# Three dilated attention patterns as one hand-ordered stream of blocks on TensorE, with projections as filler and the merge cut into steps

## The chip, the cores and the metric

The kernel runs on one core of a Trainium2 chip. Five engines work side by side, each through its own queue in order: TensorE (PE in the profile, with PEld for its weight loads), VectorE (DVE), ScalarE (ACT), GpSimd (POOL) and SyncE (SP, which here only issues DMA transfers). The metric is the device time of one execution in microseconds. The kernel before took 1517.27 us, the median of three runs (1516.05 to 1521.16).

## The reference

The kernel computes one hybrid encoder block on 1024 positions of width 1024 in float32. Two attention mixers share one input projection; the change touches the first of them, a mixture of three dilated windows over 8 heads of width 64. Cut to what matters:

```python
DIL_PATTERNS = ((128, 1), (512, 4), (2048, 16))
h = rmsnorm(x, g_mix) * (1 + scale1) + shift1
qa, ka, va, qb, kb, vb, ga, gb = split(h @ w_in)          # ga, gb: the gates
for window, dilation in DIL_PATTERNS:                     # per head
    s = q k^T / 8 + bias ;  m = max(s) ;  p = exp(s - m) ;  l = sum(p)
    o_g = (p / l) v ;  lse_g = m + log(l)
w = softmax over g of lse_g
oa = sum over g of w_g * o_g
ob = neighbourhood attention of qb, kb, vb                # mixer B, 8 heads
merged = sigmoid(ga) * (oa @ w_branch_dil) + sigmoid(gb) * (ob @ w_branch_na)
x = x + gate1 * (merged @ w_out)
# then a convolutional feed-forward layer and the final norm
```

## The kernel before

Positions are stored in the order of their residue modulo 4, so that a dilation of 4 is a contiguous run. The pattern with dilation 4 and the one with dilation 16 are evaluated together on that order (the "near" blocks: 4 residues r, each with 256 queries in two groups g); the pattern with dilation 1 is evaluated on 8 blocks of 128 neighbouring positions, 32 from each residue (the "far" blocks, in four pairs (0,7), (1,2), (3,4), (5,6)). Each float32 product is made of fp32r parts: an operand is split in a high part (ACT) and the rest (DVE or POOL), so a projection of one 128-column tile over 512 positions is 24 matmuls (`product`, lines 77 to 79: 8 values of k times 3). For the scores the two parts of q lie on the two halves of the partitions, and k's high part `ks` and rest `kl` are copied from one half of the partitions to the other by DMA (`k_copies`, line 498) once both halves of a k tile are there. `q_blocks` (line 474) brings q into the block order on POOL.

The heads are handled two at a time ("pairs"). `attend_dil` computes for each head of a pair: scores S into PSUM (lines 609, 610, 639, 640), the bias added and the minimum found by DVE (593), the exponential with its sum by ACT (594), the transposes of P on TensorE (616, 654), the split of the transposed P (ACT 598, DVE 599), the products with V (623, 669), and the evacuation of O (565, 566). Two PSUM buffers hold S, two T, two O and two the projections. After both heads the near and the far results are merged (lines 676 to 711): 16 tiny DVE copies bring the near minima and sums into block order (679), factors are computed on 16 columns (683 to 692), 16 more copies take the near factor back (696), ACT widens each factor (700), TensorE transposes it (704), DVE multiplies (706), POOL adds (710) and SP stores the result (711).

Around it stand the projections of the next pair (`qk_tiles`) and of the gates (`gate_tile`), whose weights SP loads (60), ACT and POOL split (55, 56). In the program they stand behind a pair: `counts = (2, 2, 2, 2, 1, 1, 0, 6)` gate tiles behind each of the eight pairs (four dilated, four of mixer B) and one q and one k tile. The order in which each engine runs all this is not the program's: outside blocks marked `manual_schedule` a planner takes, for each engine, what its own simulated time says is ready, the earlier in the program first. So gate and q/k matmuls come between attention matmuls where the planner finds a hole. The first q and k tiles are made before the first pair, in halves q, k, q, k.

Of the kernel before, what the change touches and what calls it, by code (L numbers as in the profile page):

```python
# [28 lines left out]
def hybrid_encoder(tc, xT, c, w_ada, small, w_in, w_v, p1_bias, p23_bias, na_bias, ln2_mult, ident, w_br, w_out,  # L29
# [406 lines left out]
    def qk_tiles(br, pr, ws=None):  # L436
        qt, kt = ((0, 4), (12, 16))[br]
# [5 lines left out]
        def q_half(hf, w, p=None):  # L443
            cols = halves[hf]
            if p is None:
                p = ps_g.tile([128, 512], FT, name="pj")
                if br == 0:
                    product(p, w, lambda k: h[hf, k])
                else:
                    q_windows(p, w, hf)  # L450
            for i in range(2):
                a, b = slice(64 * i, 64 * i + 64), slice(64 - 64 * i, 128 - 64 * i)
                d, pp = qs[i][:, cols], p
                if br:
                    d = qs[i].rearrange("p (v r t) -> p v r t", v=64, r=4)[:, :, 2 * hf:2 * hf + 2]
                    pp = p.rearrange("p (r v t) -> p v r t", r=2, v=64)
                act.activation(d[a], pp[a], AF.Copy)
                dve.tensor_tensor(d[b], pp[a], f(d[a]), OP.subtract)

        def q_windows(p, w, hf):  # L460

            whi, wlo = w
            for k in range(KT):
                mhi, mlo = (t.rearrange("p (r w c t) -> p r c w t", r=2, w=16, c=4) for t in h[hf, k])
                for x, (ww, m) in enumerate(((whi, mhi), (whi, mlo), (wlo, mhi))):
                    for r in range(2):
                        pe.matmul(p[:, 256 * r:256 * r + 256], ww[:, k], m[:, r], start=k + x + r == 0,  # L467
                                  stop=k == KT - 1 and x == 2, skip_group_check=True)

# [9 lines left out]
        def k_half(hf, w, p=None):  # L479
            cols = halves[hf]  # L480
            if p is None:
                p = ps_g.tile([128, 512], FT, name="pj")
                product(p, w, lambda k: h[hf, k])
# [16 lines left out]
        if ws:  # L500
            for hf in range(2):
                q_half(hf, ws[0])
                k_half(hf, ws[1])
            k_copies()
            q_blocks()
        else:
            w = weights(w_in[qt + pr], pool)
            for hf in range(2):
                q_half(hf, w)
            if br == 0:  # L510
                q_blocks()
            w = weights(w_in[kt + pr], pool)
            for hf in range(2):
                k_half(hf, w)
            k_copies()
        return qs, ks, kl, qb
# [45 lines left out]
    qk = qk_tiles(0, 0, qk_w)  # L562
# [14 lines left out]
    def attend_dil(pr, qk, work):  # L577
        qs, ks, kl, qb = qk
        u = [work.tile([128, S], FT, name=n) for n in ("u1", "u23")]
        st = sm_pool.tile([128, 2, 4, 8], FT, name="st")  # L580
        for i in range(2):
            head = 2 * pr + i
            a = slice(64 * i, 64 * i + 64)
            bt, vv = early_inputs.pop(0) if early_inputs else dil_inputs(head)

            def window(t, t0, n=1):

                if t0 is None:
                    return t.rearrange("p (r x t) -> p x r t", r=4, x=16)[:, 0:16:15]
                return t.rearrange("p (r t) -> p r t", r=4)[:, :, t0:t0 + 32 * n].rearrange("p r (c t) -> p c r t", c=n)  # L590

            def softmax(d, bias, pp, mi, li):
                dve.tensor_tensor_reduce(pp, d, bias, -1.0, BIG, OP.add, OP.min, mi)  # L593
                act.activation(pp, pp, AF.Exp, bias=mi, scale=-1.0, accum_out=li)  # L594

            def split_t(pt):
                th, tl = work.tile([128, 512], FR, name="th", bufs=3), work.tile([128, 512], FR, name="tl", bufs=3)
                act.activation(th, pt, AF.Copy)  # L598
                dve.tensor_tensor(tl, pt, f(th), OP.subtract)  # L599
                return th, tl  # L600

            for r in range(4):
                s = ps_l.tile([128, 512], FT, name="S")
                P = sm_pool.tile([128, 2, 256], FT, name="P", bufs=5)
                for g in range(2):
# [6 lines left out]
                    softmax(d, bt[:, 640 - 128 * g:896 - 128 * g], P[:, g], st[:, i, 2, e:e + 1], st[:, i, 3, e:e + 1])  # L612
                pt = ps_a.tile([128, 512], FT, name="T")
                for kc in range(2):
                    for g in range(2):
                        pe.transpose(pt[:, 256 * kc + 128 * g:256 * kc + 128 * g + 128],
                                     P[:, g, 128 * kc:128 * kc + 128], idt)
                tt = split_t(pt)
                if r % 2 == 0:
                    po = ps_a.tile([128, 512], FT, name="O")  # L620
                for kc in range(2):
                    for x_, t in enumerate(tt):
                        pe.matmul(po[:, 256 * (r % 2):256 * (r % 2) + 256], vv[:, 2 * r + kc],
                                  t[:, 256 * kc:256 * kc + 256], start=kc == 0 and x_ == 0, stop=kc == 1 and x_ == 1)
                if r % 2:
                    dst = u[1][a, 256 * r - 256:256 * r + 256]
                    finish_o(po, dst)

            at = {}
            po = [None, None]  # L630
            for n, bs in enumerate(((0, 7), (1, 2), (3, 4), (5, 6))):
                s = ps_l.tile([128, 512], FT, name="S")
                P = sm_pool.tile([128, 2, 256], FT, name="P", bufs=5)
                for x_, b in enumerate(bs):
                    (t0, t1), off = block_chunks(b)
                    d = s[:, 256 * x_:256 * x_ + 256]
                    mid = t0 is not None and t1 is not None
                    for dd, *keys in [(d, t0, 2)] if mid else [(d[:, 0:128], t0), (d[:, 128:256], t1)]:
                        pe.matmul(dd, qb[i][:, 128 * b:128 * b + 128], window(ks[i], *keys), start=True, stop=False)
                        pe.matmul(dd, qb[i][:, 128 * b:128 * b + 128], window(kl[i], *keys), start=False, stop=True)  # L640
                    softmax(d, bt[:, off:off + 256], P[:, x_], st[:, i, 0, b:b + 1], st[:, i, 1, b:b + 1])
                    at[b] = P[:, x_]
                if n == 0:
                    continue
                grp = ((0, 8, 1), (2, 3), (4, 5), (6, 7))[n - 1] if n < 3 else (4, 5, 6, 7)
                for js in ([grp] if n < 3 else [(4, 5), (6, 7)]):
                    pt = ps_a.tile([128, 512], FT, name="T")
                    c0, where = 0, {}
                    for j in js:
                        where[j] = c0  # L650
                        for b in (j - 1, j):
                            if 0 <= b < 8:
                                o = 128 * (j - b if 0 < b < 7 else (b, j) in ((0, 0), (7, 7)))
                                pe.transpose(pt[:, c0:c0 + 128], at[b][:, o:o + 128], idt)
                                c0 += 128
                    tt = split_t(pt)
                    for j in js:
                        ch = 15 if j in (0, 8) else 7 + j
                        own_b = [b for b in (j - 1, j) if 0 <= b < 8]
                        parts = [own_b] if own_b[0] // 4 == own_b[-1] // 4 else [[own_b[0]], [own_b[1]]]  # L660
                        for part in parts:
                            z = part[0] // 4
                            fresh = po[z] is None
                            if fresh:
                                po[z] = ps_a.tile([128, 512], FT, name="O")
                            c0 = where[j] + 128 * (part[0] - own_b[0])
                            w = 128 * len(part)
                            for x_, t in enumerate(tt):
                                pe.matmul(po[z][:, 128 * (part[0] % 4):128 * (part[0] % 4) + w], vv[:, ch],
                                          t[:, c0:c0 + w], start=fresh and x_ == 0, stop=False,  # L670
                                          skip_group_check=True)
            for z in range(2):
                dst = u[0][a, 512 * z:512 * z + 512]
                finish_o(po[z], dst)

        xs = work.tile([128, 2, 2, 8], FT, name="xs")
        for r in range(4):
            for q in range(4):
                dve.tensor_copy(xs[32 * r:32 * r + 32, :, :, q:8:4], st[32 * q:32 * q + 32, :, 2:4, 2 * r:2 * r + 2])
# [3 lines left out]
        dve.tensor_tensor(fl, st[:, :, 0], xs[:, :, 0], OP.min)  # L683
        dve.tensor_tensor(fa[:, 0], fl, st[:, :, 0], OP.subtract)
        dve.tensor_tensor(fa[:, 1], fl, xs[:, :, 0], OP.subtract)
        act.activation(fa, fa, AF.Exp)
        dve.tensor_tensor(fb[:, 0], fa[:, 0], st[:, :, 1], OP.mult)
        dve.tensor_tensor(fb[:, 1], fa[:, 1], xs[:, :, 1], OP.mult)
        dve.tensor_tensor(fl, fb[:, 0], fb[:, 1], OP.add)
        dve.reciprocal(fl, fl)  # L690
        for g in range(2):
            dve.tensor_tensor(fa[:, g], fa[:, g], fl, OP.mult)
        fx = work.tile([128, 2, 8], FT, name="fx")
# [914 lines left out]
```

## Time and profile before

| | |
|---|---|
| median of the runs | 1517.27 us |
| the profiled execution | 1523.47 us, its span 1521.7 us |
| TensorE clock granted, mean | 0.989 |
| TensorE matmul, busy | 1481.5 us, 97% |
| TensorE weight load, busy | 1252.9 us, 82% |
| VectorE, busy | 956.1 us, 63% |
| ScalarE, busy | 807.4 us, 53% |
| GpSimd, busy | 779.5 us, 51% |

The page of the profile gives busy time by engine, the span in 40 slices, the chain of work that ended last, and the groups of instructions with their idle time and its releaser. Rows of a table of stretches carry, after start and end, the length and then busy time and count for PE, PEld, DVE, ACT and POOL, the granted clock, the DMA share and GB/s. Rows of a timeline carry start, duration, engine, line, operation, output and inputs; a bracket tells the idle time before and what ended it. Matmuls are pipelined: the duration of one is longer than the distance between two starts.

### The profile page before, as it was taken

The page shows a single profiled execution, that of the slowest core. Times are in us where ns is not written, and L with a number is a line of the kernel's source. Part 1 is how long each engine was busy: PE and PEld are TensorE (multiplying, and loading weights), DVE is VectorE, ACT ScalarE, POOL GpSimd, SP SyncE. Part 2 cuts the span into 40 slices and gives each one's busy share as a digit, 9 for nine tenths or more (in the row PEclk, how much of TensorE's full clock was granted, in tenths as well). Part 3 has the DMA queues.
Part 4 walks back from the last instruction along what each step waited for, and adds up shares of the span by engine and source line. Part 5 has one row for each costly group of instructions (what it writes and reads, how often), then busy time and mean ns, then how long its engine had stood idle before and what let it go on. Part 6 is the DMA issues. An engine that isn't in the chain of part 4 may idle for free.

```text
span 1521.7 us, 21142 instructions
## 1 busy us (share of the span) xinstructions
PE 1481.5 (97%) x7512; PEld 1252.9 (82%) x7512; DVE 956.1 (63%) x1855; ACT 807.4 (53%) x1470; POOL 779.5 (51%) x506
## 2 busy tenths in 40 slices
PE   6899999999999999999999999999999999999998
PEld 5778888888888998888888878888888888778787
DVE  6664466676767665535424687665666667777765
ACT  5543566665766666644344664444444447476542
POOL 3524433333224434412156799766667675778621
PEclk8999999999999999999999999999999999999998
DMA  9857334423344655546634222222222225513323
GB/s 341 342 202 265 87 103 123 108 79 110 115 106 133 170 137 154 180 137 236 208 118 145 97 86 95 98 73 93 87 87 94 75 82 180 197 59 127 116 56 112
DMA packets 110306, 205.99 MB, mean 135 GB/s; under 512 B 40276, under 2 KB 55508, under 8 KB 110164
## 3 DMA queue, kind: packets, MB, share of 16 engines
q1 hardware_dynamic: 109928, 204.38, 41.3%
q8 instruction: 59, 0.97, 0.3%
q14 instruction: 47, 0.39, 0.1%
q10 hardware_dynamic: 272, 0.26, 0.0%
HBM read 159.51 MB, written 42.47 MB: 133 GB/s over the span
## 4 chain that ended last, share of the span: by engine, by line
PE 75%; DVE 7%; POOL 5%; ACT 4%; DMA 4%; issue 4%; SPq 0%; DVEq 0%; POOLq 0%; ACTq 0%
PE pj L79 11%; PE pj L77 11%; PE pj L78 11%; PE pj L956 8%; PE pj L954 8%; PE pj L955 8%; PE pj L467 2%; DMA wraw<-w_down 2%; PE O L768 2%; POOL wsl L56 2%; PE b L247 1%; PE b L248 1%; PE b L249 1%; PE T L756 1%; PE S L735 1%
## 5 line engine op out<-in xcount | busy, mean ns | idle before, releaser
L56 POOL TENSOR_TENSOR wlo<-wraw,whi 128x1024 fp32r<-128x1024 f32 (+1 forms) x80 | 186.6, 2333 | 229.6 <-ACT whi L55 228.2
L79 PE MATMUL pj<-h,wlo 128*128 128x512 f32 x448 | 178.0, 397 | 0.0
L78 PE MATMUL pj<-h,whi 128*128 128x512 f32 x448 | 178.0, 397 | 0.0
L77 PE MATMUL pj<-h,whi 128*128 128x512 f32 x448 | 177.8, 397 | 0.0
L1176 DVE SCALAR_TENSOR_TENSOR big<-pj,sm,big 128x512 f32<-128x512 f32 (+2 forms) x258 | 132.9, 566 | 33.3 <-ACT big L1170 32.4
L56 POOL TENSOR_TENSOR wsl<-big,wsh 128x1024 fp32r<-128x1024 f32 (+1 forms) x44 | 105.1, 2388 | 41.6 <-ACT wsh L55 41.5
L55 ACT ACTIVATE whi<-wraw 128x1024 fp32r<-128x1024 f32 (+1 forms) x80 | 82.1, 1026 | 81.0 <-PE pj L78 40.7
L1170 ACT ACTIVATE big<-pj,sm 128x512 f32<-128x512 f32 x86 | 66.5, 775 | 93.4 <-DVE pj L967 50.5
L79 PEld LDWEIGHTS pj<-h,wlo 128*128 128x128 f32 x448 | 84.3, 188 | 14.4
L78 PEld LDWEIGHTS pj<-h,whi 128*128 128x128 f32 x448 | 84.3, 188 | 14.0
L77 PEld LDWEIGHTS pj<-h,whi 128*128 128x128 f32 x448 | 84.3, 188 | 13.8
L538 POOL TENSOR_TENSOR vv<-vv 96x256 fp32r<-96x256 f32 (+2 forms) x32 | 41.2, 1297 | 98.0 <-ACT vv L537 74.4
L594 ACT ACTIVATE P<-P,st 128x256 f32<-128x256 f32 x128 | 64.5, 505 | 50.8 <-DVE st L593 50.5
L593 DVE CUSTOM_DVE_ANT_0 P<-S,bias 128x256 f32<-128x256 f32 x128 | 52.4, 421 | 43.2 <-PE S L640 24.2
L746 POOL TENSOR_SCALAR P<-P,stb 128x288 f32<-128x288 f32 (+1 forms) x32 | 40.0, 1249 | 66.9 <-DVE stb L743 53.7
L55 ACT ACTIVATE wsh<-big 128x1024 fp32r<-128x1024 f32 (+1 forms) x44 | 44.3, 1007 | 50.8 <-POOL big L889 25.5
L56 POOL TENSOR_TENSOR wsl<-wraw,wsh 128x768 fp32r<-128x768 f32 (+1 forms) x22 | 48.1, 2186 | 36.4 <-ACT wsh L55 35.2
L474 POOL TENSOR_SCALAR qb<-qs 128x256 fp32r<-128x256 f32 x32 | 26.4, 851 | 71.8 <-PE S L640 59.0
L599 DVE TENSOR_TENSOR tl<-T,th 128x512 fp32r<-128x512 f32 x64 | 43.7, 688 | 23.3 <-ACT th L598 22.8
L972 DVE TENSOR_TENSOR pj<-pj,wc 128x512 f32<-128x512 f32 x34 | 23.6, 695 | 43.9 <-PE pj L956 43.8
L79 PE MATMUL pj<-mhi,wlo 128*128 128x512 f32 x128 | 50.0, 391 | 0.4 <-POOL wlo L56 0.4
L78 PE MATMUL pj<-mlo,whi 128*128 128x512 f32 x128 | 50.0, 391 | 0.0
(395 smaller groups left out, 4755.8 us busy)
## 6 DMA issues: line engine op xcount, KB each, us to landing
t<-w_ada SPq DMA_DIRECT2D x40, 512.0 KB, 6.5
wraw<-w_in SPq DMA_DIRECT2D x32, 512.0 KB, 5.7
big<-w_up SPq DMA_DIRECT2D x22, 512.0 KB, 4.9
wraw<-w_up SPq DMA_DIRECT2D x22, 512.0 KB, 3.5
as<-big SPq DMA_DIRECT2D x22, 512.0 KB, 2.6
big<-as SPq DMA_DIRECT2D x22, 512.0 KB, 6.3
wraw<-w_down SPq DMA_DIRECT2D x24, 384.0 KB, 4.2
gs<-gs SPq DMA_DIRECT2D x32, 256.0 KB, 2.0
```

The lines of the kernel that those rows point to most:

```text
L55: act.activation(hi, raw, AF.Copy)
L56: lo_eng.tensor_tensor(lo, raw, f(hi), OP.subtract)
L77: pe.matmul(psum, whi[:, k0 + k], mhi, start=k == 0, stop=False)
L78: pe.matmul(psum, whi[:, k0 + k], mlo, start=False, stop=False)
L79: pe.matmul(psum, wlo[:, k0 + k], mhi, start=False, stop=k == n - 1)
L593: dve.tensor_tensor_reduce(pp, d, bias, -1.0, BIG, OP.add, OP.min, mi)
L594: act.activation(pp, pp, AF.Exp, bias=mi, scale=-1.0, accum_out=li)
L954: pe.matmul(psum, whi[:, k], bhi, start=j < 4 and i == 0, stop=False, skip_group_check=True)
L955: pe.matmul(psum, whi[:, k], blo, start=False, stop=False, skip_group_check=True)
L956: pe.matmul(psum, wlo[:, k], bhi, start=False, stop=i == n - 1, skip_group_check=True)
L1170: act.activation(y[:, halves[hf]], src, AF.Identity, bias=conv[:, 3, t:t + 1], scale=conv[:, 1, t:t + 1])
L1176: dve.scalar_tensor_tensor(y[:, dst], src, wt, y[:, dst], OP.mult, OP.add)
```

## The change

`attend_dil` is split. `dil_head` returns, for one head, eight units: a block's scores, and behind it the "turn" (transposes and split) and the "values" (products with V and the evacuation) that may run later. `qk_parts` and `gate_part` become generators that give up control after every third matmul. `attend_dils` then writes the order of the four pairs out by hand: 16 slots a pair (23 for the last). A slot has the scores of one block, a step of the previous pair's merge, a third of its quota of filler, the transposes of an earlier block, another third, the values of a block before that, and the last third. The filler is one stream: two gate tiles, then for each next pair its q tile, its k tile and two gate tiles (for mixer B's first pair one), each tile's weights being loaded as the one before it starts. The whole stands in a `manual_schedule` block for TensorE, so that TensorE runs it in program order; the other engines stay with the planner. V and bias of a later head are loaded at the fifth slot of a head, and `q_blocks` of a pair is called in its first slot.

The merge becomes a generator of 11 steps, one a slot, from slot 12 of a pair to slot 6 of the next. The 16 copies into block order run on ACT. The factors of both patterns stay in block order, so the 16 copies back are gone; instead the near result is read and written through a view in block order, and DVE does the addition (a product into PSUM and a sum) in place of POOL. Nine gate tiles stand in the dilated part in place of eight, two behind mixer B's first pairs, five at the end in place of six.

```diff
-        for r in range(4):
-            for q in range(4):
-                dve.tensor_copy(xs[32 * r:32 * r + 32, :, :, q:8:4], st[32 * q:32 * q + 32, :, 2:4, 2 * r:2 * r + 2])
...
-        for r in range(4):
+        def copies(r):
             for q in range(4):
-                dve.tensor_copy(fx[32 * q:32 * q + 32, :, 2 * r:2 * r + 2], fa[32 * r:32 * r + 32, 1, :, q:8:4])
...
-        for z in range(2):
+                act.activation(xs[32 * r:32 * r + 32, :, :, q:8:4],
+                               st[32 * q:32 * q + 32, :, 2:4, 2 * r:2 * r + 2], AF.Copy)
+
+        def exponents():
+            dve.tensor_tensor(fl, st[:, :, 0], xs[:, :, 0], OP.min)
+            dve.tensor_tensor(fa[:, 0], fl, st[:, :, 0], OP.subtract)
+            dve.tensor_tensor(fa[:, 1], fl, xs[:, :, 0], OP.subtract)
+            act.activation(fa, fa, AF.Exp)
+
+        def factors():
+            dve.tensor_tensor(fb[:, 0], fa[:, 0], st[:, :, 1], OP.mult)
+            dve.tensor_tensor(fb[:, 1], fa[:, 1], xs[:, :, 1], OP.mult)
+            dve.tensor_tensor(fl, fb[:, 0], fb[:, 1], OP.add)
+            dve.reciprocal(fl, fl)
+            for g in range(2):
+                dve.tensor_tensor(fa[:, g], fa[:, g], fl, OP.mult)
...
+        def scale(z, g):
             dst = u[1].rearrange("p (r b j) -> p b r j", r=4, b=8)[:, 4 * z:4 * z + 4]
-            src = u[0][:, 512 * z:512 * z + 512].rearrange("p (b r j) -> p b r j", b=4, r=4)
-            pool.tensor_tensor(dst, dst, src, OP.add)
-        sp.dma_start(o_scr[0][pr], u[1])
+            src = u[0][:, 512 * z:512 * z + 512]
+            pt = ps_a.tile([128, 512], FT, name="T")
+            for b in range(4):
+                pe.transpose(pt[:, 128 * b:128 * b + 128], fws[z, g][:, b], idt)
+            view = pt.rearrange("p (b r j) -> p b r j", b=4, r=4)
+            if g:
+                dve.tensor_tensor(dst, dst, view, OP.mult)
+            else:
+                dve.tensor_tensor(pt, src, pt, OP.mult)
+                dve.tensor_tensor(dst, dst, view, OP.add)
...
+        zg = ((0, 1), (0, 0), (1, 1), (1, 0))
+        yield from [[lambda r=r: copies(r)] for r in range(4)]
+        yield [exponents]
+        yield [factors]
+        yield [lambda: wide_factor(*zg[0])]
+        for n in range(4):
+            steps = [lambda n=n: scale(*zg[n])]
+            if n < 3:
+                steps.append(lambda n=n: wide_factor(*zg[n + 1]))
+            else:
+                steps.append(store)
+            yield steps
...
+    def attend_dils(qk, work):
+
+
+        pairs = {0: (qk, None)}
+        tiles = [(24 + t, gate_part(t)) for t in range(2)]
+        gates = itertools.count(2)
...
+        for n in range(1, 5):
+            qt, kt = ((0, 4), (12, 16))[n // 4]
+            tiles += [(qt + n % 4, part_of(n, 2)), (kt + n % 4, part_of(n, 3))]
+            for _ in range(2 if n < 4 else 1):
+                t = next(gates)
+                tiles.append((24 + t, gate_part(t)))
+
+        def filler():
+            w = weights(w_in[tiles[0][0]], pool)
+            for i, (_, part) in enumerate(tiles):
+                now = w
+                if i + 1 < len(tiles):
+                    w = weights(w_in[tiles[i + 1][0]], pool)
+                yield from part(now)
...
+        inputs, turns, valued, merges = list(early_inputs), [], [], []
+        for n in range(4):
+            u = [work.tile([128, S], FT, name=t) for t in ("u1", "u23")]
+            st = sm_pool.tile([128, 2, 4, 8], FT, name="st")
+            quota = ([4] * 8 if n == 0 else [4, 4, 3, 3, 2, 3, 3, 2]) + [5, 5, 6, 5, 5, 6, 4, 4]
+            for slot in range(16 if n < 3 else 23):
+                i, x_ = divmod(slot, 8)
+                if x_ == 0 and slot < 16:
+                    units = dil_head(i, pairs[n][0], u, st, *inputs.pop(0), work)
+                k = quota[slot] if slot < 16 else 2
+                ks = [k // 3 + (k % 3 > 0), k // 3 + (k % 3 > 1), k // 3]
+                after = []
+                if slot < 16:
+                    units[x_][0]()
+                    after = units[x_][1]
+                if slot == 0 and n:
+                    pairs[n][1][4]()
+                if slot == 12:
+                    merges.append(merging(n, u, st, work))
+                if merges:
+                    for step in next(merges[0], ()):
+                        step()
+                run(ks[0])
+                now = turns.pop(0) if turns else None
+                if now:
+                    now[0]()
+                run(ks[1])
+                if valued:
+                    valued.pop(0)()
+                if now:
+                    valued.append(now[1])
+                turns += after
+                if x_ == 4 and slot < 16 and 0 < 2 * n + i < 7:
+                    inputs.append(dil_inputs(2 * n + i + 1))
+                run(ks[2])
+                if merges and slot in (6, 22):
+                    merges.pop(0)
+        through_all(fill)
...
-        counts = (2, 2, 2, 2, 1, 1, 0, 6)
...
+        with tc.manual_schedule(engines={pe.engine}):
+            qk, gates = attend_dils(qk, work)
+        for hv in range(2):
+            vb_chunks(slice(hv * 256, hv * 256 + 256))
+        counts = (1, 1, 0)
```

More of the change, by code (lines that the diff above doesn't have):

```diff
@@ L434, in hybrid_encoder, with stream, through_all, qk_parts @@
     ps_g = tc.alloc_tile_pool(name="psg", bufs=2, space=PSUM, reuse_waits="tile")
-    def qk_tiles(br, pr, ws=None):
-        qt, kt = ((0, 4), (12, 16))[br]
+    def stream(p, w, moving):
+        for k in range(KT):
+            product(p, w, moving, ks=[k])
+            yield
+    def through_all(gen):
+        for _ in gen:
+            pass
+    def qk_parts(br, pr):
         qs = [qkpool.tile([128, S], FR, name="qs") for _ in range(2)]
@@ L441, in qk_tiles, with q_half @@
         qb = []
-        def q_half(hf, w, p=None):
+        def q_half(hf, w):
             cols = halves[hf]
[L445 to L450, printed above, removed]
+            p = ps_g.tile([128, 512], FT, name="pj")
+            if br == 0:
+                yield from stream(p, w, lambda k: h[hf, k])
+            else:
+                yield from q_windows(p, w, hf)
             for i in range(2):
@@ L575, in block_chunks, with dil_head @@
         return (32 * b - 16, 32 * b + 16), 128
-    def attend_dil(pr, qk, work):
+    def dil_head(i, qk, u, st, bt, vv, work):
         qs, ks, kl, qb = qk
[L579 to L600, printed above, removed]
-            for r in range(4):
@@ new lines, in dil_head, with window, softmax @@
+        a = slice(64 * i, 64 * i + 64)
+        def window(t, t0, n=1):
+            if t0 is None:
+                return t.rearrange("p (r x t) -> p x r t", r=4, x=16)[:, 0:16:15]
+            return t.rearrange("p (r t) -> p r t", r=4)[:, :, t0:t0 + 32 * n].rearrange("p r (c t) -> p c r t", c=n)
+        def softmax(d, bias, pp, mi, li):
+            dve.tensor_tensor_reduce(pp, d, bias, -1.0, BIG, OP.add, OP.min, mi)
+            act.activation(pp, pp, AF.Exp, bias=mi, scale=-1.0, accum_out=li)
@@ L603, in attend_dil, with split_t, near, scores @@
+        def split_t(pt):
+            th, tl = work.tile([128, 512], FR, name="th", bufs=3), work.tile([128, 512], FR, name="tl", bufs=3)
+            act.activation(th, pt, AF.Copy)
+            dve.tensor_tensor(tl, pt, f(th), OP.subtract)
+            return th, tl
+        po, at, tts, own = [None, None], {}, {}, {}
+        def near(r):
+            def scores():
                 s = ps_l.tile([128, 512], FT, name="S")
-                P = sm_pool.tile([128, 2, 256], FT, name="P", bufs=5)
+                P = own[r] = sm_pool.tile([128, 2, 256], FT, name="P", bufs=5)
@@ L627, in attend_dil @@
[L627 to L671, printed above, removed]
@@ L672, in attend_dil, with far_scores @@
-            for z in range(2):
-                dst = u[0][a, 512 * z:512 * z + 512]
-                finish_o(po[z], dst)
+                    finish_o(own["o"], u[1][a, 256 * r - 256:256 * r + 256])
+            return scores, turn, values
+        def far_scores(bs):
+            s = ps_l.tile([128, 512], FT, name="S")
+            P = sm_pool.tile([128, 2, 256], FT, name="P", bufs=5)
+            for x_, b in enumerate(bs):
+                (t0, t1), off = block_chunks(b)
+                d = s[:, 256 * x_:256 * x_ + 256]
+                mid = t0 is not None and t1 is not None
+                for dd, *keys in [(d, t0, 2)] if mid else [(d[:, 0:128], t0), (d[:, 128:256], t1)]:
+                    pe.matmul(dd, qb[i][:, 128 * b:128 * b + 128], window(ks[i], *keys), start=True, stop=False)
+                    pe.matmul(dd, qb[i][:, 128 * b:128 * b + 128], window(kl[i], *keys), start=False, stop=True)
+                softmax(d, bt[:, off:off + 256], P[:, x_], st[:, i, 0, b:b + 1], st[:, i, 1, b:b + 1])
+                at[b] = P[:, x_]
@@ new lines, in far, with turn, values @@
+        def far(n, js):
+            where = {}
+            def turn():
+                pt = ps_a.tile([128, 512], FT, name="T")
+                c0 = 0
+                for j in js:
+                    where[j] = c0
+                    for b in (j - 1, j):
+                        if 0 <= b < 8:
+                            o = 128 * (j - b if 0 < b < 7 else (b, j) in ((0, 0), (7, 7)))
+                            pe.transpose(pt[:, c0:c0 + 128], at[b][:, o:o + 128], idt)
+                            c0 += 128
+                tts["far", n] = split_t(pt)
+            def values():
+                for j in js:
+                    ch = 15 if j in (0, 8) else 7 + j
+                    own_b = [b for b in (j - 1, j) if 0 <= b < 8]
+                    parts = [own_b] if own_b[0] // 4 == own_b[-1] // 4 else [[own_b[0]], [own_b[1]]]
+                    for part in parts:
+                        z = part[0] // 4
+                        fresh = po[z] is None
+                        if fresh:
+                            po[z] = ps_a.tile([128, 512], FT, name="O")
+                        c0 = where[j] + 128 * (part[0] - own_b[0])
+                        w = 128 * len(part)
+                        for x_, t in enumerate(tts["far", n]):
+                            pe.matmul(po[z][:, 128 * (part[0] % 4):128 * (part[0] % 4) + w], vv[:, ch],
+                                      t[:, c0:c0 + w], start=fresh and x_ == 0, stop=False, skip_group_check=True)
+                if n > 1:
+                    z = n - 2
+                    finish_o(po[z], u[0][a, 512 * z:512 * z + 512])
+            return turn, values
@@ L676, in attend_dil, with merging @@
+        nears = [near(r) for r in range(4)]
+        fars = [far(n, js) for n, js in enumerate(((0, 8, 1), (2, 3), (4, 5), (6, 7)))]
+        return [(nears[r][0], [nears[r][1:]]) for r in range(4)] + \
+            [(lambda bs=bs: far_scores(bs), after) for bs, after in
+             (((0, 7), []), ((1, 2), fars[:1]), ((3, 4), fars[1:2]), ((5, 6), fars[2:]))]
+    def merging(pr, u, st, work):
         xs = work.tile([128, 2, 2, 8], FT, name="xs")
-        for r in range(4):
-            for q in range(4):
-                dve.tensor_copy(xs[32 * r:32 * r + 32, :, :, q:8:4], st[32 * q:32 * q + 32, :, 2:4, 2 * r:2 * r + 2])
@@ L682, in attend_dil @@
         fl = work.tile([128, 2, 8], FT, name="fl")
[L683 to L690, printed above, removed]
@@ new lines, in gate_part, with part, part_of, run @@
+    def gate_part(t):
+        def part(w):
+            for hf, cols in enumerate(halves):
+                p = ps_g.tile([128, 512], FT, name="pj")
+                yield from stream(p, w, lambda k: h[hf, k])
+                g = gspool.tile([128, 512], FT, name="gs")
+                act.activation(g, p, AF.Copy)
+                sp.dma_start(g_scr[t][:, cols], g)
+        return part
+    def attend_dils(qk, work):
+        pairs = {0: (qk, None)}
+        tiles = [(24 + t, gate_part(t)) for t in range(2)]
+        gates = itertools.count(2)
+        def part_of(n, which):
+            def part(w):
+                if n not in pairs:
+                    made = qk_parts(n // 4, n % 4)
+                    pairs[n] = made[0], made
+                return pairs[n][1][which](w)
+            return part
+        for n in range(1, 5):
[11 more added lines that the diff above has]
+                yield from part(now)
+        fill = filler()
+        def run(n):
+            for _ in range(n):
+                next(fill, None)
+        inputs, turns, valued, merges = list(early_inputs), [], [], []
[36 more added lines that the diff above has]
+        through_all(fill)
+        assert not turns and not valued and not merges
+        return pairs[4][0], next(gates)
```

101 lines of the change are left out of this document (48 added, 53 removed).

## The prediction

> **What bounds the kernel now.** I read the page first: span and busy time.
>
> ```profile
> span 1521.7 us, 21142 instructions
> PE 1481.5 (97%) x7512; PEld 1252.9 (82%) x7512; DVE 956.1 (63%) x1855; ACT 807.4 (53%) x1470; POOL 779.5 (51%) x506
> ```
>
> TensorE (PE) is busy for nearly the whole span, so the end moves only if PE loses less time between matmuls. The same matmuls run before and after (one gate tile moves from the end into the dilated stage, a merge keeps its 16 transposes for each pair), so I look for PE's lost time, not for work. The dilated stage lies between about 164 and 470 us. Next, the table of stretches: us, busy time and count of PE, weight loads, DVE, ACT, POOL, then granted clock, DMA share, GB/s.
>
> ```profile
> 320.00:360.00 40.00, 39.76 (x239) 34.70 (x238) 26.20 (x71) 26.34 (x67) 16.33 (x12) 1.00 0.34 98
> 360.00:400.00 40.00, 36.75 (x261) 34.27 (x260) 28.49 (x86) 23.26 (x56) 13.07 (x10) 0.96 0.35 103
> 387.60:391.00 3.40, 3.40 (x19) 3.40 (x18) 2.86 (x8) 2.63 (x8) 0.00 (x0) 0.50 0.61 141
> 960.00:1000.00 40.00, 40.00 (x178) 33.14 (x177) 25.46 (x43) 17.59 (x21) 27.53 (x17) 1.00 0.23 80
> ```
>
> In the pure projection stretch (960 to 1000) 178 matmuls of 512 columns fill 40 us: 0.225 us each, the price of a matmul here. In 360 to 400 PE lost 3.25 us outright, and for 3.4 us after that the clock was 0.50: about half of them, 1.7 us, is lost as well. Then the waits of the weight loads, which stand ahead of each matmul, from 160 to 640 us (total, times, longest).
>
> ```profile
> PEld S L609 <- DVE st L593: 3.3, 5, 2.2
> PEld S L735 <- DVE stb L739: 2.8, 2, 1.5
> PEld S L639 <- DVE st L593: 2.6, 3, 1.7
> PEld O L669 <- DVE tl L599: 1.1, 1, 1.1
> PEld O L623 <- DVE tl L599: 1.0, 4, 0.3
> PEld O L623 <- ACT th L598: 0.6, 3, 0.3
> PEld T L616 <- ACT P L594: 0.2, 1, 0.2
> PEld T L616 <- DVE u L706: 0.2, 1, 0.2
> ```
>
> They sum to 11.8 us, and 8.7 of them are score matmuls that wait for a late softmax on DVE (S is double buffered). What DVE does then is seen at the worst of them:
>
> ```profile
> 379.73 2.38 POOL L56 TENSOR_TENSOR wlo<-wraw,whi 128x1024 fp32r<-128x1024 f32 x1
> 382.06 1.01 POOL L558 TENSOR_TENSOR bias<-bias,lnm 128x384 f32<-128x384 f32 x1
> 379.91 3.19 DVE L692 TENSOR_TENSOR fa<-fa,fl 128x16 f32<-128x16 f32 x2
> 383.14 2.79 DVE L696 COPY fx<-fa 32x4 f32<-32x4 f32 x16
> 385.95 0.42 DVE L593 CUSTOM_DVE_ANT_0 P<-S,bias 128x256 f32<-128x256 f32 x1
> ```
>
> From 379.9 to 385.9 DVE works only on the merge of a pair: two 16-column products last 3.19 us, ending as POOL's two operations end (382.06 + 1.01 = 383.07), then 16 tiny copies. The softmax comes 6 us late and PE stands.
>
> **Part 1, the merge.** These rows group the dilated stage's merge operations:
>
> ```profile
> L679 DVE COPY xs<-st 32x8 f32<-32x8 f32 x64 | 20.8, 324 | 7.8 <-ACT P L594 6.9
> L696 DVE COPY fx<-fa 32x4 f32<-32x4 f32 x64 | 12.5, 195 | 1.0
> L706 DVE TENSOR_TENSOR u<-u,T 128x512 f32<-128x512 f32 x16 | 10.9, 684 | 1.2 <-PE T L704 1.1
> L692 DVE TENSOR_TENSOR fa<-fa,fl 128x16 f32<-128x16 f32 x8 | 7.3, 956 | 0.1
> L686 ACT ACTIVATE fa<-fa x4: 218/220/227, 233.0 to 449.3; 128x32 f32<-128x32 f32 x4
> ```
>
> DVE loses all 128 copies, 33.3 us or 8.3 a pair, and gains two 512-column operations a pair (2 x 0.684 = 1.4 us) for POOL's two additions. ACT gains 16 small copies a pair; none runs on ACT before, the nearest row is L686 at 0.22 us for 128x32, so 16 x 0.22 = 3.5 us, bounds 0 (overlapped with neighbours) to 16 x 0.32 = 5.2 us (L679's mean). All of it is beside PE; ACT is busy 26 of 40 us, so it hides. The worth is that DVE no longer holds a burst: one step a slot, in 11 slots of some 4 us. The removable loss is the 11.8 us of waits and the 1.7 us at half clock, 13.5 us.
>
> How much stays? A slot is a block of scores (4 matmuls), a group of transposes (4), a group of values (4) and 2 to 6 filler units of 3 matmuls of 0.225 us. Attention matmuls start 0.12 us apart:
>
> ```profile
> 175.64 0.28 PE L610 MATMUL S<-kl,qs 128*128 128x256 f32 x1
> 175.76 0.28 PE L609 MATMUL S<-ks,qs 128*128 128x256 f32 x1
> ```
>
> So a slot lasts 12 x 0.12 = 1.4 us plus 1.4 to 4.1 us. Transposes come at least a slot after their scores, values a slot after their transposes. What must fit into that slot:
>
> ```profile
> L594 ACT ACTIVATE P<-P,st 128x256 f32<-128x256 f32 x128 | 64.5, 505 | 50.8 <-DVE st L593 50.5
> L593 DVE CUSTOM_DVE_ANT_0 P<-S,bias 128x256 f32<-128x256 f32 x128 | 52.4, 421 | 43.2 <-PE S L640 24.2 <-PE S L610 17.4
> L599 DVE TENSOR_TENSOR tl<-T,th 128x512 fp32r<-128x512 f32 x64 | 43.7, 688 | 23.3 <-ACT th L598 22.8
> L598 ACT ACTIVATE th<-T 128x512 fp32r<-128x512 f32 x64 | 37.6, 591 | 9.9 <-PE T L654 6.4 <-PE T L616 3.0
> ```
>
> The chain is 0.42 + 2 x 0.51 = 1.4 us for scores, 0.59 + 0.69 = 1.3 us for transposes, against 3 to 4 us of cover. Waits of 0 to 11.8 us stay; I take 2.3, a fifth, since the chain fills under half of the cover. Gain: 13.5 - 2.3 = **11.2 us**.
>
> **Part 2, the start of the stream.** In program order TensorE's first work after the first q and k tiles is a block of scores, ahead of any filler. Those scores read both halves of ks and kl, which SP's copies (L498) fill after the last half of k. Before, PE ran the next pair's q tile meanwhile:
>
> ```profile
> 163.90 0.39 PE L79 MATMUL pj<-h,wlo 128*128 128x512 f32 x1
> 164.13 0.39 PE L77 MATMUL pj<-h,whi 128*128 128x512 f32 x1
> 165.87 0.49 SPq L498 DMA_DIRECT2D ks<-ks  x1
> 166.59 0.47 SPq L498 DMA_DIRECT2D kl<-kl  x1
> 169.57 0.40 PE L609 MATMUL S<-ks,qs 128*128 128x256 f32 x2
> DMA to landing us min/median/max: 2.9/4.8/6.7
> ```
>
> 163.90 is the 96th and last matmul of the first q and k; from 164.13 on it is filler that the changed order no longer has there. The kl copy of head 0, issued at 166.59, lands 2.9 to 6.7 us later, at 169.5 to 173.3, so PE stands for 5.4 to 9.2 us. I take 3.5 us, near the low end since only one copy is ahead of it, and so 6.0 us. The gap at 384 to 386 shows what follows: a stretch at 0.50. Of its 3.4 us some falls into the standstill, so 1.2 us more, between 0 and 1.7. Cost: **7.2 us**. The queue behind that score matmul is all of PE's; what waits for it is the gate tiles and so ACT and DVE, which have slack.
>
> The Trainium skill (TensorE: Matmul & The Clock Gate, Why this matters for your kernels) asks for no PE gap over about 3 us, or the clock falls to half. This trace is harsher, since a 2.2 us wait was followed by 0.50. By the rule the old gap would have cost no clock, and the change would gain 1.7 us less while the start pays the same.
>
> **Part 3, the other pair boundaries.** k of the next pair ends two slots before that pair. Cover: 8 units x 0.675 + 2 x 1.4 = 8.2 us. Need, from the same step before:
>
> ```profile
> 199.62 0.39 PE L79 MATMUL pj<-h,wlo 128*128 128x512 f32 x1
> 201.56 0.47 SPq L498 DMA_DIRECT2D kl<-kl  x1
> ```
>
> 201.56 + 2.9 to 6.7 less 199.85 is 4.6 to 8.4 us, so 0 to 0.2 us each; I take 0. Without the cover each would cost the 6 us of the start. SP must not hold those copies behind a V load; the diff places the loads two slots earlier.
>
> **Part 4, the end.** 272 units of filler are gone by slot 19 of the last pair, and three merge steps are left: 12 transposes behind 0.68 us products. If nothing of the next stage may go between, up to 2 us; its scores have been ready since unit 256, so 0. The gate tile that moves costs nothing in sum.
>
> **Sum.** 11.2 - 7.2 = 4.0 us gained. The profiled execution took 1523.47 us (span 1521.7) against a median of 1517.27; the difference is carried over, 1519.5 for a profiled run, **1513.3** for the median.
>
> **Rivals.** *A: the start is covered* (copies land early or other PE work gets ahead of the scores). For it: in the stretch before, nothing else waits for those copies. Against: program order. Time 1517.3 - 11.2 = 1506.1.
>
> *B: slower, DVE and POOL in slots 0 and 1.* The reorder of q (eight L474 operations) is now issued in slot 0 of each pair, just where exponents() and factors() put eight small two-operand operations on DVE.
>
> ```profile
> L474 POOL TENSOR_SCALAR qb<-qs 128x256 fp32r<-128x256 f32 x24 | 19.8, 852 | 71.8 <-PE S L640 59.0 <-issue 12.8
> ```
>
> If each of the eight waits for one POOL operation as L692 did, DVE is late by 8 x 0.85 = 6.8 us. It decides once the lateness exceeds the slot of cover, 4.2 us: 2.6 us at PE plus 1.7 at half clock, in each of three pairs 12.9 us, so 1513.3 + 12.9 = 1526.2. Against: POOL's reorder is only needed four slots later and may be spread. The Trainium skill (SBUF — State Buffer, Who interferes with whom) says that a DVE instruction with two SBUF inputs is shut out for the whole of a GpSimd instruction that reads SBUF, and that ACT never is; the 3.19 us row agrees. By it the copies are safe on ACT, and B is what remains.
>
> *C: the change does not do what it says*, the order of the other engines, still planned, is late for PE's fixed one and the waits only move to transposes and values: 6.5 of the 11.8 us stay, 13.5 - 6.5 = 7.0 us pays for the start, 1517.5. For it: DVE and ACT are busy 26 of 40 us, so queues form. Against: the cover of two to three times the chain.
>
> **How the numbers follow.** Forecast 0.45, A 0.25, B 0.17, C 0.13. A measurement of this kernel tells 0.3%, 4.6 us, from no change, and the forecast of 4.0 lies close to that edge: I count half of it as faster, half as same (0.22 and 0.23). A is faster; C is same but for 0.02 slower; B is slower. Faster 0.47, same 0.34, slower 0.19. The forecast's own range is 1508 to 1518 (waits that stay 0 to 6, start 5.4 to 9.2); with A's 1506 less an even smaller rest and B short of its full price, 1503 to 1525.
>
> **What would show it.** Right: PE idle for 5 to 9 us before the first L609-like score at about 164 to 170, released by a DMA, with a clock of 0.50 behind; few weight-load waits on the softmax after that; no tiny copies on DVE; no dip of the clock near 385. Wrong: filler between first k and first scores (A); DVE merge operations stretched to 0.8 us or more right beside L474's and PE waiting in the first slots of a pair (B); waits of the size of before spread over T and O (C).

## The result, and the profile after

The changed kernel takes 1584.24 us in the median of four runs, against 1519.22 us for the kernel before on the same chip: a ratio of 1.0416 with a 95% interval of 1.0399 to 1.0433. It is slower by 4.2%, some 65 us, where a gain of 4 us was forecast and a range up to 1525 us was given. The profiled execution took 1585.35 us (span 1583.5).

The page has the same 7512 matmuls, and TensorE's share has fallen.

```profile
span 1583.5 us, 21030 instructions
PE 1498.5 (95%) x7512; PEld 1257.8 (79%) x7512; DVE 928.7 (59%) x1735; ACT 830.1 (52%) x1534; POOL 769.0 (49%) x498
```

The table of stretches (start and end, length, busy time and count for PE, PEld, DVE, ACT, POOL, then clock, DMA share, GB/s) shows where: in the hand-ordered part, evenly, and behind it only a little near 740 us.

```profile
200.00:240.00 40.00, 35.20 (x190) 29.30 (x190) 15.64 (x43) 24.07 (x65) 11.47 (x8) 1.00 0.21 65
240.00:280.00 40.00, 34.40 (x197) 28.73 (x196) 19.53 (x58) 22.64 (x54) 11.16 (x8) 1.00 0.39 102
440.00:480.00 40.00, 34.18 (x237) 30.31 (x236) 20.49 (x54) 25.02 (x65) 6.51 (x3) 1.00 0.43 126
520.00:560.00 40.00, 40.00 (x272) 36.96 (x271) 28.89 (x71) 26.16 (x58) 17.90 (x14) 1.00 0.43 127
720.00:760.00 40.00, 38.06 (x184) 31.21 (x184) 15.06 (x25) 17.85 (x30) 4.74 (x2) 0.96 0.42 146
```

In the stream TensorE stands for 5 to 6 us of every 40, at the full clock, while DVE and ACT do less than before. The stage's last store of dilated results (SP's issue of `oa<-u`) moves from 473.3 to 535.7 us. The waits of the weight loads from 160 to 640 us name one cause (total, times, longest):

```profile
PEld S L659 <- DVE st L608: 29.0, 32, 1.6
PEld S L627 <- DVE st L608: 28.5, 32, 1.5
PEld S L627 <- issue: 5.0, 1, 5.0
PEld S L871 <- DVE tl L614: 1.2, 1, 1.2
PEld S L628 <- DMA kl<-kl: 1.1, 1, 1.1
PEld T L675 <- issue: 0.2, 1, 0.2
```

The first two rows have 32 waits each: 4 near and 4 far blocks of 8 heads, 64 in all, one for every block, 57.5 us together. L627 and L659 are the scores. The waits on transposes and values, on which the prediction dwelt, have all but gone: none stands in the list beside 0.2 us. One block on TensorE and VectorE, from the timelines:

```profile
342.28 0.39 PE L79 MATMUL pj<-h,wlo 128*128 128x512 f32 x1
342.51 0.28 PE L627 MATMUL S<-ks,qs 128*128 128x256 f32 x1
342.63 0.28 PE L628 MATMUL S<-kl,qs 128*128 128x256 f32 x1
343.54 0.38 PE L627 MATMUL S<-ks,qs 128*128 128x256 f32 x1 [0.64 <-DVE st L608]
343.76 0.28 PE L628 MATMUL S<-kl,qs 128*128 128x256 f32 x1
343.88 0.40 PE L77 MATMUL pj<-h,whi 128*128 128x512 f32 x1
```

```profile
343.05 0.43 DVE L608 CUSTOM_DVE_ANT_0 P<-S,bias 128x256 f32<-128x256 f32 x1 [1.10 <-PE S L628]
343.40 0.08 DVE L608 DVE_READ_ACCUMULATOR2_ANT st<- 128x1 f32 x1
344.08 0.42 DVE L608 CUSTOM_DVE_ANT_0 P<-S,bias 128x256 f32<-128x256 f32 x1 [0.59 <-PE S L628]
```

A block has two groups of scores, here two matmuls each. The first group starts at 342.51, VectorE reads it from 343.05 to 343.48, and only then, at 343.54, does the second group start, 0.91 us after the matmul before it where 0.12 us would do. VectorE is not late here: it had been idle for 1.10 us. The program calls the softmax inside the loop over the two groups, and both groups are halves of one PSUM tile, so the second group's matmuls wait for the reader of the first. TensorE's projections stand behind them in its queue.

The kernel before has the same two loops. There the planner filled the gap. It also mixes blocks, so that two groups which follow each other in its trace need not belong together; the far block of the pair (0, 7) can be told apart, since of all scores its alone come as products of 128 columns, four to a group:

```profile
213.69 0.22 PE L639 MATMUL S<-ks,qb 128*128 128x128 f32 x1
...
214.73 0.31 PE L640 MATMUL S<-kl,qb 128*128 128x128 f32 x1
214.88 0.44 PE L77 MATMUL pj<-h,whi 128*128 128x512 f32 x1
215.16 0.28 PE L639 MATMUL S<-ks,qb 128*128 128x256 f32 x1
...
219.40 0.39 PE L79 MATMUL pj<-h,wlo 128*128 128x512 f32 x1
219.62 0.22 PE L639 MATMUL S<-ks,qb 128*128 128x128 f32 x1
```

```profile
216.70 0.42 DVE L593 CUSTOM_DVE_ANT_0 P<-S,bias 128x256 f32<-128x256 f32 x1
```

Its first group ends with the matmul at 214.73, VectorE reads it from 216.70 to 217.12, and its second group starts at 219.62. Between the two groups stand the first group of another block (215.16), some transposes and 18 projection matmuls.

The start of the stream looks as forecast. In the first row below (waits of TensorE itself) it waits for the copy of ks, then for that of kl; the stretch behind is at half clock.

```profile
PE S L627 <- DMA ks<-ks: 4.6, 1, 4.6
PE S L628 <- DMA kl<-kl: 0.8, 1, 0.8
```

```profile
170.00:174.00 4.00, 3.84 (x10) 3.16 (x11) 0.54 (x4) 1.20 (x4) 0.00 (x0) 0.50 0.46 143
```

And the merge has done what it was to do: no tiny copy is left on VectorE, the copies on ScalarE take what L686 suggested, and the 16-column products no longer stretch (0.172 us where they were 0.956).

```profile
L715 ACT ACTIVATE xs<-st 32x8 f32<-32x8 f32 x64 | 13.7, 214 | 1.1
```

```profile
L730 DVE TENSOR_TENSOR fa<-fa,fl 128x16 f32<-128x16 f32 x8 | 1.0, 172 | 0.1
```

### The profile page after: what moved, and what is told of

It reads as the page before. It is cut to its first block, busy times and chain, and to the rows that moved or that the text cites. A ratio compares the mean times of both kernels' runs of the same rounds, so it can differ in the third digit from the quotient of the medians.

```text
span 1583.5 us, 21030 instructions
## 1 busy us (share of the span) xinstructions
PE 1498.5 (95%) x7512; PEld 1257.8 (79%) x7512; DVE 928.7 (59%) x1735; ACT 830.1 (52%) x1534; POOL 769.0 (49%) x498
## 4 chain that ended last, share of the span: by engine, by line
PE 73%; DVE 8%; ACT 6%; POOL 5%; DMA 4%; issue 3%; SPq 1%; DVEq 0%; ACTq 0%; POOLq 0%
PE pj L78 10%; PE pj L77 10%; PE pj L79 9%; PE pj L1088 9%; PE pj L1087 9%; PE pj L1086 9%; PE pj L475 3%; PE O L904 2%; DVE P L608 1%; POOL wsl L56 1%; PE T L892 1%; POOL wlo L56 1%; PE S L871 1%; PE b L247 1%; PE b L248 1%
## 5 line engine op out<-in xcount | busy, mean ns | idle before, releaser
L77 PE MATMUL pj<-h,whi 128*128 128x512 f32 x448 | 183.7, 410 | 0.0
L78 PE MATMUL pj<-h,whi 128*128 128x512 f32 x448 | 177.7, 397 | 0.0
L609 ACT ACTIVATE P<-P,st 128x256 f32<-128x256 f32 x128 | 64.8, 507 | 80.6 <-DVE st L608 80.1
L896 DVE TENSOR_TENSOR tl<-T,th 96x512 fp32r<-96x512 f32 (+1 forms) x48 | 32.7, 684 | 37.4 <-ACT th L895 33.9
L613 ACT ACTIVATE th<-T 128x512 fp32r<-128x512 f32 x64 | 38.1, 595 | 24.7 <-PE T L636 12.8
```

The costliest lines, as they stand in the source:

```text
L77: pe.matmul(psum, whi[:, k0 + k], mhi, start=k == 0, stop=False)
L78: pe.matmul(psum, whi[:, k0 + k], mlo, start=False, stop=False)
```

## The experiments

The theory, W: the 64 waits follow from the order of the program, in which the second group of a block writes the PSUM tile that VectorE still reads for the first; with TensorE in program order nothing covers them. The rivals: D, VectorE and ScalarE are late in general because they are still planned while TensorE is fixed; M, the new merge or the slots themselves cost the time.

**Scores ahead of the softmaxes.** In the changed kernel, the two groups' matmuls of a block are issued before its two softmaxes; the far blocks likewise.

```diff
                     pe.matmul(d, qs[i][:, qc], kl[i][:, kc], start=False, stop=True)
+                for g in range(2):
+                    d = s[:, 256 * g:256 * g + 256]
                     e = 2 * r + g
                     softmax(d, bt[:, 640 - 128 * g:896 - 128 * g], P[:, g], ...)
```

> The changed kernel, but in each block all four score matmuls stand ahead of the two softmaxes (near and far); nothing else differs. Theory W (the second group of a block writes the PSUM tile that VectorE is still reading for the first group, so in program order TensorE stands in every one of the 64 blocks): the 57.5 us of weight-load waits of L627 and L659 on the softmax go, 45 to 57 us are gained, 1527 to 1540 us. Rival D (VectorE and ScalarE are late as such, because their order is planned and TensorE's is fixed): the waits move to the transposes and the time stays above 1570 us.

1517.92 us, a ratio of 0.998 (0.9966 to 0.9995) to the kernel before: 66 us less than the changed kernel, more than the 45 to 57 us that W gave. The waits of the weight loads from 150 to 760 us are down to the start and some small ones behind the attention:

```profile
PEld S L627 <- issue: 5.0, 1, 5.0
PEld pj L77 <- ACT o1hi L55: 1.2, 2, 0.8
PEld S L628 <- DMA kl<-kl: 1.1, 1, 1.1
PEld pj L77 <- DVE g L991: 0.6, 2, 0.3
PEld pj L78 <- DVE o1lo L56: 0.5, 1, 0.5
PEld pj L79 <- POOL wlo L56: 0.3, 1, 0.3
```

```profile
200.00:240.00 40.00, 40.00 (x229) 34.42 (x228) 19.48 (x52) 28.06 (x73) 13.88 (x9) 1.00 0.25 69
240.00:280.00 40.00, 40.00 (x248) 35.17 (x248) 23.34 (x71) 27.13 (x70) 12.48 (x9) 1.00 0.60 173
```

Behind the start TensorE no longer stands in the stream. Rival D falls: the waits did not move to the transposes.

**The order kept, a tile for each group.** The softmaxes stay where they are, but each group gets a PSUM tile of its own, from the same two buffers.

```diff
-                s = ps_l.tile([128, 512], FT, name="S")
...
-                    d = s[:, 256 * g:256 * g + 256]
+                    d = ps_l.tile([128, 256], FT, name="S")
```

> The changed kernel in its own order of scores and softmaxes, but each group of scores in a PSUM tile of its own, one bank each, from the same two buffers. Theory W in its narrow form (the wait is for the bank that VectorE reads, not for anything in the order of scores and softmaxes): as fast as with the scores first, 1515 to 1522 us. Rival: the wait is for VectorE's result or its place in the queue, or the two buffers now collide from block to block: above 1550 us.

1521.54 us, a ratio of 1.0003 (0.9991 to 1.0015). In its trace no score waits for a softmax:

```profile
PEld S L626 <- issue: 5.0, 1, 5.0
PEld S L627 <- DMA kl<-kl: 1.2, 1, 1.2
```

```profile
320.00:360.00 40.00, 40.00 (x249) 35.14 (x246) 23.11 (x61) 29.58 (x77) 9.85 (x6) 1.00 0.28 87
```

So the order alone does little harm; it is the tile shared by writer and reader. The 3.6 us against the scores first do not lie in the scores: in the profiled execution the values of mixer B wait at 676 us (L902 for `th`, 1.7 us), and the clock is near 0.50 from 677.3 to 684.2 us. It needs no more PSUM, since the two buffers now hold two groups in place of two blocks, and a slot is long enough for that.

**The wait kept and covered.** One or two of the slot's filler units are issued between the two groups.

```diff
                 for g in range(2):
+                    if g:
+                        between()          # run(two): two units, one where the slot has only two
                     d = s[:, 256 * g:256 * g + 256]
```

> The changed kernel with the softmaxes left where they are, but one or two of the slot's filler units moved between the two groups of scores (0.7 or 1.4 us of TensorE work). Theory W: the wait is still there and is covered, 35 to 55 us are gained, 1529 to 1550 us; where only one unit stands between, 0.2 to 0.5 us a block remain. Rival D: no gain, above 1570 us.

1523.36 us, a ratio of 1.0011 (1.0001 to 1.0022): 61 us less than the changed kernel, where 35 to 55 were expected, with the softmaxes still between the groups. What remains of the waits is short:

```profile
PEld S L663 <- DVE st L608: 5.6, 9, 0.8
...
PEld S L629 <- DVE st L608: 1.7, 4, 0.5
```

13 waits in place of 64. The wait is real and is hidden by 0.7 to 1.4 us of projections, as the planner did it.

**TensorE back with the planner.** Only the `manual_schedule` around the stream is taken away.

> The changed kernel without the hand order: TensorE goes back to the planner, all else (spread merge, generators, slots) stays. Theory W: the planner puts projections between the two groups of a block as it did before, so the time falls to 1510 to 1530 us. Rival M (the new merge or the slot structure is what costs): it stays above 1560 us.

1511.74 us, 0.9934 (0.9919 to 0.9949). Rival M falls too: merge, generators and slots stay, and the time is below that of the kernel before.

**The old kernel with the scores first.** The same edit of the two loops in the kernel before.

> The kernel before with the same reordering of scores and softmaxes. Theory W: before, the planner already covered most of this wait, and only the 5.9 us that L609 and L639 waited for the softmax can go: 0 to 6 us faster, 1513 to 1519 us. Rival D: no difference.

1511.04 us, 0.9932 (0.9917 to 0.9947), 10 us less than the kernel before where at most 6 were expected. The waits of L609 and L639 on the softmax are gone; what is left from 160 to 640 us hangs on the split behind the transposes:

```profile
PEld O L674 <- DVE tl L599: 2.6, 4, 1.3
PEld O L625 <- DVE tl L599: 1.5, 1, 1.5
```

These waits in the kernel before were therefore of the same kind: the second half of a block, caught behind the first half's softmax when VectorE was busy with the merge. Why the gain is 10 us and not 6 is only partly seen: the waits of mixer B on VectorE (2.8 us) are gone from the list as well, and so is the stretch at half clock: the clock is 1.00 from 160 to 480 us.

**The start filled.** On the changed kernel with the scores first, eight filler units of the first eight slots are issued ahead of the first block.

```diff
+        run(8)
...
-            quota = ([4] * 8 if n == 0 else [4, 4, 3, 3, 2, 3, 3, 2]) + [5, 5, 6, 5, 5, 6, 4, 4]
+            quota = ([3] * 8 if n == 0 else [4, 4, 3, 3, 2, 3, 3, 2]) + [5, 5, 6, 5, 5, 6, 4, 4]
```

> The changed kernel with the scores ahead of the softmaxes, and eight of the filler units of the first eight slots (one of each slot's four) moved ahead of the first block of scores. Theory W with the start as the only other loss: the 5.4 us in which TensorE waited for the copies of ks and kl and the half clock behind it go, 6 to 8 us are gained on the kernel without the filler at the start (1517.9), 1510 to 1512 us. Rival: the copies are slower than eight units (5.4 us) or the gate weights are not there yet, so 2 us or more stay.

1509.31 us, 0.9917 (0.9903 to 0.9932). Set against the 0.998 without it, that is 0.6%, some 9 us; the profile of the stretch from 160 to 200 us, without and with it:

```profile
160.00:200.00 40.00, 34.56 (x173) 28.89 (x172) 12.92 (x39) 18.86 (x45) 10.07 (x7) 0.91 0.29 86
```

```profile
160.00:200.00 40.00, 39.59 (x223) 33.85 (x222) 15.27 (x51) 24.61 (x68) 8.97 (x6) 1.00 0.36 108
```

50 matmuls more fit into the same 40 us; 0.7 us of waiting for kl remains in the list of waits.

**A gate tile back at the end.** `counts = (1, 0, 0)` in place of `(1, 1, 0)` on the kernel just shown.

> The one before it with one gate tile less behind mixer B's second pair and six at the end in place of five, as the kernel before had them. If the gate tiles at the end cover the way from the last attention output to the branch projections, 1 to 4 us less than the run before it; if five are enough, no difference.

1510.84 us, 0.9924 (0.9911 to 0.9936): no difference. Five gate tiles at the end are enough.

**Planner and scores first.** The changed kernel with the scores first and no `manual_schedule`.

> The changed kernel with the scores ahead of the softmaxes and TensorE back with the planner. If the hand order is worth something once the bank wait and the start are mended, this is slower than the hand-ordered kernel with the start filled (1509.3); if the planner does as well, 1505 to 1510 us; if the spread of the merge over slots is what the planner lacks, 1503 to 1506 us.

1507.85 us, 0.9912 (0.9897 to 0.9926), against 0.9917 for the mended hand order. The two intervals lie on each other: the hand order is worth nothing that these runs can tell.

**The new merge alone.** The kernel before with the scores first, and `merging` in place of the old merge, all steps at its place, ordered by the planner.

```diff
+        for steps in merging(pr, u, st, work):
+            for step in steps:
+                step()
```

> The kernel before with the scores ahead of the softmaxes, and with the new merge (copies on ScalarE, factors in block order, sum on VectorE), all its steps called where the old merge stood and ordered by the planner. Theory: the merge's burst on VectorE costs TensorE 3 to 6 us there, which the new merge takes away: 1506 to 1509 us against 1511.0 with the old merge. Rival: once the bank wait is gone the merge is covered by projections and the new one gains nothing, 1510 to 1512 us.

1504.64 us, 0.9888 (0.9875 to 0.9902): 1.1% faster than the kernel before and the fastest of all by the medians. Against the same kernel with the old merge (0.9932) the new merge is worth 0.44%, 6.7 us, a little more than expected. Against the hand order with its start filled (0.9917) the intervals only just part (0.9902 and 0.9903), and the traces show no difference: from 160 to 520 us TensorE is idle for 0.4 us in both. From 160 to 640 us its weight loads wait once, for half a microsecond:

```profile
PEld pj L77 <- PE S L702: 0.5, 1, 0.5
```

**Copies on VectorE again.** The kernel just shown, with the 16 copies into block order as `dve.tensor_copy`.

> The kernel before with the scores first and the new merge, but with the 16 copies into block order of each pair on VectorE again. If the gain of the new merge (1511.0 to 1504.6) lies in taking them off VectorE, where a GpSimd operation holds one for up to 2.3 us, half of it or more goes: 1508 to 1511 us. If it lies in the 16 copies back that are gone and in the sum off GpSimd, it stays: 1504 to 1506 us.

1507.94 us, 0.9921 (0.9906 to 0.9936). By the medians most of the merge's gain is gone; the trace does not bear it out. The copies take 14.2 us on VectorE at 0.222 us each, and of the weight loads from 150 to 640 us only these wait:

```profile
PEld pj L77 <- PE S L702: 0.6, 1, 0.6
PEld O L800 <- ACT th L791: 0.4, 1, 0.4
```

The two profiled spans differ by 1.4 us (1504.9 and 1503.5), less than the medians, whose 3.3 us these two executions do not show. Where the rest lies was not found, and how the merge's gain divides between the moved copies and the dropped ones stays open.

## Why the prediction was wrong

**What bounds the kernel: right in kind, wrong in one reading.** The time did follow from what TensorE loses between matmuls. But the list of weight-load waits was read as the price of a late softmax, of the kind that a spread merge takes away, with the remark that S is double buffered. Each of the two buffers holds a whole block, so the two groups of a block share one. With the scores first, the rows L609 and L639 on the softmax's minimum are gone from the kernel before: they were second groups of blocks, waiting for the reader of the first.

**Part 1, "how much stays": the step that failed.** The chain was set against the cover between scores and transposes and between transposes and values, and both were right: those waits vanished. The dependency inside a block, two calls of the softmax between two pairs of matmuls on one tile, was not in the list of chains at all. It was to be seen in the loop, and in the trace before, where 4.9 us and 18 projections lie between the two groups of block (0, 7). In program order it has no cover: the slot's filler comes behind both groups. "2.3 us stay" became 57.5 us in the weight loads, 0.90 us in each of 64 blocks, of which 44.9 us are seen as idle TensorE. The range did not hold it either: the bound of 11.8 us was the sum of the waits that the planner had left, and a wait that is covered does not show in such a list at all. (By their own bounds, 1517.3 - 13.5 + 5.4 and 1517.3 - 7.5 + 9.2, the forecast's own range comes to 1509 to 1519 and not 1508 to 1518, which changes nothing here.)

The Trainium skill (PSUM — Partial Sum Buffer, PSUM bank collisions raise a hardware error) says that the hardware does not hold back a TensorE write into a bank which another engine reads, but raises an error, so that the program has to keep the two apart. The trace agrees in that the matmul waits for VectorE's semaphore; a tile for each group takes the wait away (1521.5 us). No run here shows the error itself.

**Part 1, the merge: right in kind, too large in size.** The copies cost ScalarE 0.214 us against an estimate of 0.22, VectorE's burst is gone, and the new merge is worth 6.7 us where the planner orders TensorE. The 11.2 us set down for it were in part the block wait, which the merge only exposed: the kernel before gains 10 us by the order of its loops alone.

**Part 2, the start: right, with the clock undersized.** 6.0 us of standstill and 1.2 us of lost clock were forecast; the trace has 4.6 + 0.8 us of waits for the copies with a short block wait behind, and the clock at 0.50 from 167.2 to 174.0 us, in which TensorE is busy for 4.97 us, so that some 2.5 us are lost. Filling it gained some 9 us against 7.2.

**Parts 3 and 4: right but for the last boundary.** No later dilated pair waits for its k copies in the changed kernel. The first scores of mixer B, put at nothing because they had been ready, wait once for kl, 1.0 us, and the clock falls behind it. The moved gate tile costs nothing.

**The rivals.** B, VectorE shut out by the reorder of q, did not happen: the small products ran at 0.172 us. A was ruled out by the trace. C named the right kind of cause, TensorE's fixed order against the planner's, but at another place and at a far smaller size. With the one loop mended the changed kernel takes 0.998 of the time of the kernel before, some 3 us less. That this is near the forecast 4.0 confirms no term of the sum, since the mended loop alone is worth 10 us in the kernel before.

The 66 us between it and the changed kernel are more than the 57.5 us of waits in the weight loads. The profiled spans differ by 67.6 us (1583.5 and 1515.9), and the trace accounts for nearly that: in the 64 blocks the second group starts 0.99 us in the mean behind the matmul before it, where 0.12 us would do, and its second matmul 0.22 us behind its first in place of 0.12, some 62 us together. The rest lies at two waits that the mended kernel does not have, 1.0 us for kl at mixer B's first scores and 1.9 us for the values of its last pair (the loss near 740 us), each followed by 3.4 us at half clock:

```profile
508.00:511.90 3.90, 2.33 (x12) 1.75 (x11) 3.15 (x8) 1.64 (x5) 0.00 (x0) 1.00 0.97 242
511.90:515.30 3.40, 3.40 (x13) 2.72 (x12) 1.90 (x9) 1.88 (x6) 0.00 (x0) 0.50 0.71 209
740.60:744.00 3.40, 3.40 (x14) 3.01 (x14) 0.81 (x2) 1.15 (x3) 0.00 (x0) 0.50 0.02 5
```

## What to carry to other kernels

Before an engine is put in program order, list for its instructions every dependency on another engine, also those between two halves of one tile, and ask of each what stands between; a planner's order may have covered a wait so well that no list of waits shows it. Issue all writes to a PSUM tile before its first reader, or give each reader's part a tile of its own. Try the loop order under the planner first: here that gave 0.7%, the merge 0.4% more, and the hand order nothing that could be measured.

## What the runs showed of the hardware

The half clock needs no long gap in TensorE's work. In the kernel before, 0.50 from 387.6 us on followed a single wait of 2.2 us. In the changed kernel it came at 511.9 us after two gaps of 0.98 and 0.59 us, with TensorE busy for 2.33 of the 3.90 us before, and at 740.6 us after gaps of 1.52 and 0.34 us. The block waits before that, one every 5 us or so with TensorE idle for 0.5 to 1.35 us, left the clock at 1.00 from 174 to 505 us. So in these traces the idle time added up over a few microseconds goes with the half clock, and not the longest gap alone; how it is counted no run here shows.
